# Stores of y issued by ScalarE, and raw rows of the operand preparation queued behind the latest weights

## The chip, the core and the metric

The kernel runs on one core of one Trainium2 chip. The time is device microseconds of one execution of the whole program. Five engines work side by side, each from its own queue in order: TensorE (PE; PEld is its loading of weights), VectorE (DVE), ScalarE (ACT), GpSimd (POOL) and SyncE (SP), which in this kernel issues every transfer.

## What is computed

One layer of a hybrid decoder block over 2048 tokens of width 1024, in float32, followed by a gated projection of a second input p and a final norm. Cut to what matters:

```
z = rmsnorm(h, norm_mix) @ w_in                     # 1024 -> 5392 columns
aq, ak, av, gq, gk, gv, g_low, za, zg = split(z)
y_att = swa_sink_attention(rope(aq), rope(ak), av, sinks)   # 16 heads of 64, window 128
o     = gla_chunked(gq, gk, gv, logsigmoid(g_low @ w_gate_up + b_gate) / 16)  # 4 heads
y     = concat(y_att * silu(za), rmsnorm(o, gla_norm) * silu(zg))   # 2048 wide
h     = h + y @ w_out
gate  = sigmoid(rmsnorm(h, ple_norm) @ w_ple_gate)
out   = rmsnorm(h + gate * (p @ w_ple_proj), final_norm)
```

## The kernel before

Every product is split into a high and a low part of float32r, three matmuls for one (`gemm`, line 83: high by high, high by low, low by high). Hence each weight tile has two buffers, `wh` and `wl`.

The tokens are worked in two halves of eight tiles of 128. In each half the normalised input stays on the chip (`uth`, `utl`), and column groups of w_in pass by one after the other. Section A makes keys, values and the low-rank gate input of each tile. Then, for each of four GLA heads i, come `v_block`, `qk_block` and eight GLA tiles (`gla_tile`, line 549), and behind heads 0, 1 and 2 come the attention groups 0 and 1, 2, and 3, eight attention tiles each (`att_tile`, line 409). An attention tile goes from projection and rotary through scores (`s`), exponentials, transposes (`pq`) and the product with values to `oy` on VectorE (line 479), which is stored to the DRAM scratch `yts[t]` (line 480). A GLA tile ends in a transpose and ScalarE's copy to `oyg` (line 586), stored by line 587. These are 64 stores each of 128 KB.

`load_w` (line 265) brings one column group into one of two buffer slots (`wps`). In the first half raw columns come from w_in, and ScalarE and GpSimd split them into `wh` and `wl`, which are also saved to DRAM (`wd`, line 292). In the second half the saved parts come back with eight transfers, `wh` and `wl` in turn (lines 278 and 279).

Only in the second half there runs, between the tiles, the generator `right_operands` (line 597). It prepares the operands of the output products, which use a seven-product scheme for 2x2 blocks: 48 units, each with four raw rows loaded into `rb` (line 609), four differences on VectorE (`tm`), splits on ScalarE (`th`, line 625) and GpSimd (line 626), and four stores to `td` (line 628). Its tiles come from the pool `rawp` (nine buffers).

The program text gives only the order in which work is traced. The tile framework simulates the engines when the program is built and lays out each engine's queue by when it takes each instruction to be ready. `tc.issue_after(ins)` (line 607) adds a rule to that: what is traced in its block on the engine of `ins` stands behind `ins` in that engine's queue, without waiting for it to finish. `pace[0]` holds that instruction; before the change it is the store of y that was traced last (lines 480 and 587). `tick` (line 308) advances all open generators by one step between blocks of projection.

Behind the second half follow the output products (`products`, line 780) with operands `T` loaded from `td` (line 122) and y read back from `yts` (line 805).

Of the kernel before, what the change touches and what calls it, by code (L numbers as in the profile page):

```python
# [10 lines left out]
F32 = mybir.dt.float32  # L11
# [27 lines left out]
def hybrid_block_kernel(  # L39
# [5 lines left out]
    nc = tc.nc  # L45
# [4 lines left out]
    yts = [dram.tile([P, 16, P], F32, name=f"yts{t}") for t in range(NT)]  # L50
# [5 lines left out]
    def pt(tag, shape=(P, 512), dtype=F32, bufs=2):  # L56
        return psum.tile(list(shape), dtype, name=tag, tag=tag, bufs=bufs)
# [68 lines left out]
    with ExitStack() as p1:  # L126
# [27 lines left out]
        def w1(name, dtype=F32, shape=(P, 256)):  # L154
            return wk.tile(list(shape), dtype, name=name, tag="w1", bufs=8)
# [91 lines left out]
        def rope(q, nh, t):  # L247
            cb = csC[:, t, :].unsqueeze(1).broadcast_to([P, nh, 16])
            s0 = csS[:, t, 0:8].unsqueeze(1).broadcast_to([P, nh, 8])
            s1 = csS[:, t, 8:16].unsqueeze(1).broadcast_to([P, nh, 8])  # L250
            a = wk.tile([P, 4, 16], F32, name="ra", tag="ra", bufs=1)[:, 0:nh, :]
            b = wk.tile([P, 4, 16], F32, name="rb", tag="rb", bufs=1)[:, 0:nh, :]
            dve.tensor_tensor(a, q[:, :, 0:16], cb, op=ALU.mult)
            dve.tensor_tensor(b[:, :, 0:8], q[:, :, 8:16], s0, op=ALU.mult)
            dve.tensor_tensor(b[:, :, 8:16], q[:, :, 0:8], s1, op=ALU.mult)
            dve.tensor_tensor(q[:, :, 0:16], a, b, op=ALU.add)
# [4 lines left out]
        slot = [0]  # L261

        wds = {}

        def load_w(cols, fast=False):
            n = sum(c[1] for c in cols)
            wp = wps[slot[0] % 2]
            slot[0] += 1
            wh = wp.tile([P, KD, SW], F32R, name="wh", tag="wh")
            wl = wp.tile([P, KD, SW], F32R, name="wl", tag="wl")  # L270
            key = tuple(cols)
            saved = wds.get(key)
            if saved is None:
                wds[key] = dram.tile([P, 2, KD, n], F32, name=f"wd{len(wds)}")
            for k0 in range(0, KD, 2):
                ks_ = slice(k0, k0 + 2)
                if saved is not None:
                    nc.sync.dma_start(wh[:, ks_, 0:n].bitcast(F32), saved[:, 0, ks_, :])
                    nc.sync.dma_start(wl[:, ks_, 0:n].bitcast(F32), saved[:, 1, ks_, :])
                    continue  # L280
                raw = rawp.tile([P, 2, SW], F32, name="raw", tag="raw")
                o = 0
                for c0, m in cols:
                    nc.sync.dma_start(raw[:, :, o:o + m], w_v[:, ks_, c0:c0 + m])
                    o += m
                act.activation(wh[:, ks_, 0:n], raw[:, :, 0:n], AF.Copy)  # L286
                eng = dve if fast and k0 % 4 == 0 else pool
                eng.tensor_tensor(wl[:, ks_, 0:n], raw[:, :, 0:n], wh[:, ks_, 0:n], op=ALU.subtract)  # L288
            if saved is None:

                for i, part in enumerate((wh, wl)):
                    nc.sync.dma_start(wds[key][:, i], part[:, :, 0:n].bitcast(F32))
            return wh, wl

        def tok_gemm(ps, w, lt, c0, n):
            ts_ = slice(lt * P, lt * P + P)
            gemm(ps[:, 0:n], lambda k: uth[:, k, ts_], lambda k: utl[:, k, ts_],
                 lambda k: w[0][:, k, c0:c0 + n], lambda k: w[1][:, k, c0:c0 + n], KD)
# [110 lines left out]
        def att_tile(half, g, wq, lt, szas):  # L409
            kv = g // 2  # L410
            t = half * HT + lt
            ps = pt("acc")
            tok_gemm(ps, wq, lt, 0, 256)
            q = w1("q", shape=(P, 4, 64))
            act.activation(q, ps[:, 0:256].rearrange("p (h d) -> p h d", h=4), AF.Copy)
            rope(q, 4, t)
            stk = w2("stk", F32R, (P, 4, 2, 64))
            split(stk[:, :, 0, :], stk[:, :, 1, :], q)
            yield
            tp = pt("t", dtype=F32R)  # L420
            for j in range(4):
                pe.transpose(tp[:, j * P:(j + 1) * P], stk[:, j].rearrange("p a d -> p (a d)"), identr)
            qT = w2("qT", F32R, (P, 4, P))
            act.activation(qT, tp.rearrange("p (h n) -> p h n", h=4), AF.Copy)
            yield
            sp = pt("s", (P, 4, 256), bufs=1)
            win = slice(lt * P, lt * P + 256)
            for j in range(4):
                pe.matmul(sp[:, j, :], qT[:, j, :], kT[:, kv, 0, win], start=True, stop=False)
                pe.matmul(sp[:, j, :], qT[:, j, :], kT[:, kv, 1, win], start=False, stop=True)  # L430
            s = w2("s", F32, (P, 4, P))
            act.activation(s, sp[:, :, P:256], AF.Copy)
            um = umask.unsqueeze(1).broadcast_to([P, 4, P])
            if t == 0:
                dve.copy_predicated(s, um, negc.unsqueeze(2).broadcast_to([P, 4, P]))
            else:
                dve.copy_predicated(s, um, sp[:, :, 0:P])
            hsl = slice(4 * g, 4 * g + 4)
            sm = wk.tile([P, 6, 4], F32, name="sm", tag="sm", bufs=3)
            mx, ng, es, su, dn = (sm[:, i, :] for i in range(5))  # L440
            dve.tensor_reduce(out=mx, in_=s, op=ALU.max, axis=AX.X)
            dve.scalar_tensor_tensor(ng, mx, -1.0, nsk[:, hsl], op0=ALU.mult, op1=ALU.min)  # L442
            dve.tensor_tensor(es, ng, nsk[:, hsl], op=ALU.subtract)
            act.activation(es, es, AF.Exp)
            for j in range(4):
                act.activation(s[:, j, :], s[:, j, :], AF.Exp, bias=ng[:, j:j + 1], accum_out=su[:, j:j + 1])  # L446
            dve.tensor_tensor(dn, su, es, op=ALU.add)
            dve.reciprocal(dn, dn)
            dve.scalar_tensor_tensor(s, s, 0.5, dn.unsqueeze(2).broadcast_to([P, 4, P]),
                                     op0=ALU.mult, op1=ALU.mult)  # L450
            yield
            yield
            tp = pt("t")
            for j in range(4):
                pe.transpose(tp[:, j * P:(j + 1) * P], s[:, j, :], ident)
            pq = kvp.tile([P, 4, 512], F32R, name="pq", tag="pq", bufs=1)
            split(pq[:, 0, :], pq[:, 1, :], tp)
            pmb = pmask.unsqueeze(1).broadcast_to([P, 4, P])
            for i in range(2):
                pool.tensor_tensor(pq[:, 2 + i, :].rearrange("p (h n) -> p h n", h=4),  # L460
                                   pq[:, i, :].rearrange("p (h n) -> p h n", h=4), pmb, op=ALU.mult)
            yield
            yield
            po = pt("o")
            vp = vs[:, lt, kv].rearrange("p a d -> p (a d)")
            vq = vd[:, lt, kv].rearrange("p a d -> p (a d)")
            pe.matmul(po, vp, pq[:, 0, :], start=True, stop=False)
            pe.matmul(po, vp, pq[:, 1, :], start=False, stop=False)
            pe.matmul(po, vq, pq[:, 2, :], start=False, stop=False)
            pe.matmul(po, vq, pq[:, 3, :], start=False, stop=True)  # L470
            pv = po.rearrange("p (a b n) -> p a b n", a=2, b=2)
            ot = w1("ot", shape=(P, 2, P))
            act.activation(ot[0:64], pv[64:128, :, 0, :], AF.Copy)
            act.activation(ot[64:128], pv[0:64, :, 1, :], AF.Copy)
            dve.tensor_tensor(ot[0:64], ot[0:64], pv[0:64, :, 0, :], op=ALU.add)
            dve.tensor_tensor(ot[64:128], ot[64:128], pv[64:128, :, 1, :], op=ALU.add)
            oy = w1("oy", shape=(P, 2, P))
            l2 = lt % 4
            dve.tensor_tensor(oy, ot, szas[lt // 4][:, :, l2 * P:(l2 + 1) * P], op=ALU.mult)
            pace[0] = nc.sync.dma_start(yts[t][:, 2 * g:2 * g + 2, :], oy).ins  # L480


        def gla_gates(half, h, sub, res):
# [65 lines left out]
        def gla_tile(half, h, wz, lt, ops):  # L549
            t = half * HT + lt  # L550
# [33 lines left out]
                pe.transpose(tq[:, j * P:(j + 1) * P], y[:, j * P:(j + 1) * P], ident)  # L584
            oy = w1("oyg", shape=(P, 2, P))
            act.activation(oy, tq[:, 0:256].rearrange("p (a n) -> p a n", a=2), AF.Copy)
            pace[0] = nc.sync.dma_start(yts[t][:, 8 + 2 * h:10 + 2 * h, :], oy).ins

        pace = [None]

        def run_chain(c):
            next(c)
# [497 lines left out]
```

## Time and profile before

| what | value |
|---|---|
| median of 3 runs | 1906.24 us (1900.41 to 1909.64) |
| profiled execution | 1904.04 us, its span 1902.3 us |
| mean granted TensorE clock | 0.990 |
| TensorE, VectorE, ScalarE, GpSimd busy | 95%, 63%, 51%, 37% |
| transfers | 326.78 MB, mean 172 GB/s |

How to read it: busy shares are over the whole span, which has parts of different kinds; a wait is the time in which an engine stood idle, put down to what released it last. An engine that isn't the bound may stand idle at no cost. SyncE's rows are issues: the time is that of the issuing instruction, and the data lands some us later.

### The profile page before, as it was taken

Reading aid. Unit: us, or ns where it says so; the run is one execution under the profiler, and the core shown is the slowest. Engines: PE = TensorE matmul, PEld = TensorE weight load, DVE = VectorE, ACT = ScalarE, POOL = GpSimd, SP = SyncE. Lnnn points to the kernel's source line nnn. Section 1 sums busy time; section 2 is a strip of 40 time slices with the busy share of each in tenths; the row PEclk is TensorE's granted clock in tenths of the full one; section 3 lists DMA queues with packets and bytes.
Section 4 is the critical chain, followed back from the end, with each engine's and each line's share of the span. In section 5 each row is a group of like instructions: output and inputs, shape, how many; then the busy total and the mean of one; then the engine's idle time right before and its main releaser. Section 6 shows DMA issues by size and latency. Waiting matters only on the chain. (4 is left out here: it accounts for less than half of the span.)

```text
span 1902.3 us, 32715 instructions
## 1 busy us (share of the span) xinstructions
PE 1814.7 (95%) x11297; PEld 1612.9 (85%) x11297; DVE 1203.3 (63%) x2663; ACT 961.1 (51%) x2598; POOL 699.3 (37%) x916
## 2 busy tenths in 40 slices
PE   6999999999999999999999999999899999998997
PEld 6989898998898889898888988988788888787886
DVE  6454785466556474578766756574667667665864
ACT  5544666465557464456654655563422244453543
POOL 5442554534526362544455445352200010102432
PEclk9999999999999999999999999999999999999998
DMA  8332442415324352655576566565685966884542
GB/s 281 122 101 81 147 136 92 155 53 170 97 66 143 102 180 90 199 146 174 178 205 206 163 195 182 160 195 192 230 281 194 324 237 219 313 309 151 179 139 83
DMA packets 326741, 326.78 MB, mean 172 GB/s; under 512 B 23137, under 2 KB 259825, under 8 KB 326321
## 3 DMA queue, kind: packets, MB, share of 16 engines
q1 hardware_dynamic: 326576, 324.70, 52.5%
q8 instruction: 89, 1.46, 0.3%
q14 instruction: 76, 0.61, 0.1%
HBM read 186.08 MB, written 138.54 MB: 171 GB/s over the span
## 5 line engine op out<-in xcount | busy, mean ns | idle before, releaser
L85 PE MATMUL acc<-wh,uth 128*128 128x256 f32 (+1 forms) x1664 | 476.8, 287 | 14.5 <-DVE m L563 4.5
L86 PE MATMUL acc<-wl,uth 128*128 128x256 f32 (+1 forms) x1664 | 472.6, 284 | 6.2 <-DMA wl<-wd 6.0
L87 PE MATMUL acc<-wh,utl 128*128 128x256 f32 (+1 forms) x1664 | 471.1, 283 | 0.0
L85 PEld LDWEIGHTS acc<-wh,uth 128*128 128x128 f32 x1664 | 316.0, 190 | 25.6 <-ACT v L522 5.9
L86 PEld LDWEIGHTS acc<-wl,uth 128*128 128x128 f32 x1664 | 315.7, 190 | 12.9 <-DMA wl<-wd 8.6
L87 PEld LDWEIGHTS acc<-wh,utl 128*128 128x128 f32 x1664 | 315.7, 190 | 2.0
L460 POOL TENSOR_TENSOR pq<-pq,pmask 128x512 fp32r<-128x512 f32 x128 | 178.2, 1408 | 292.9 <-ACT pq L67 285.8
L85 PE MATMUL acc<-uth,wh 128*128 128x512 f32 x512 | 204.3, 399 | 4.8 <-DVE m L563 3.8
L87 PE MATMUL acc<-uth,wl 128*128 128x512 f32 x512 | 201.7, 394 | 0.3 <-DMA wl<-wd 0.3
L86 PE MATMUL acc<-utl,wh 128*128 128x512 f32 x512 | 201.9, 394 | 0.0
L774 PE MATMUL acc<-T,c 128*128 128x512 f32 (+1 forms) x344 | 135.5, 395 | 6.7 <-ACT u L829 6.3
L775 PE MATMUL acc<-T,c 128*128 128x512 f32 (+1 forms) x344 | 135.1, 393 | 0.0
L776 PE MATMUL acc<-T,c 128*128 128x512 f32 (+1 forms) x344 | 135.0, 393 | 0.0
L446 ACT ACTIVATE s<-s,sm 128x128 f32<-128x128 f32 x256 | 99.7, 391 | 51.1 <-DVE sm L442 51.1
L85 PEld LDWEIGHTS acc<-uth,wh 128*128 128x128 f32 x512 | 96.4, 188 | 26.8 <-DVE m L563 5.2
L859 POOL TENSOR_TENSOR ssh<-ssh 128x1 f32<-128x1 f32 x16 | 3.3, 205 | 313.8 <-ACT junk L858 313.8
L288 POOL TENSOR_TENSOR wl<-raw,wh 128x512 fp32r<-128x512 f32 (+1 forms) x82 | 109.6, 1367 | 20.0 <-ACT wh L286 10.2
L87 PEld LDWEIGHTS acc<-uth,wl 128*128 128x128 f32 x512 | 96.1, 188 | 22.5 <-DMA wl<-wd 0.7
L86 PEld LDWEIGHTS acc<-utl,wh 128*128 128x128 f32 x512 | 96.2, 188 | 18.7
L67 ACT ACTIVATE c<-s 128x512 fp32r<-128x512 f32 x72 | 45.1, 629 | 111.1 <-DVE s L104 32.4
L774 PE MATMUL o<-T,c 128*128 128x512 f32 (+1 forms) x252 | 99.3, 394 | 0.0
L775 PE MATMUL o<-T,c 128*128 128x512 f32 (+1 forms) x252 | 98.6, 391 | 0.0
(289 smaller groups left out, 4409.7 us busy)
## 6 DMA issues: line engine op xcount, KB each, us to landing
T<-td SPq DMA_DIRECT2D x84, 512.0 KB, 9.4
wd<-wh SPq DMA_DIRECT2D x20, 1024.0 KB, 5.6
wd<-wl SPq DMA_DIRECT2D x20, 1024.0 KB, 6.3
wh<-wd SPq DMA_DIRECT2D x80, 256.0 KB, 5.4
wl<-wd SPq DMA_DIRECT2D x80, 256.0 KB, 5.5
raw<-in_w_in SPq DMA_DIRECT2D x68, 256.0 KB, 5.6
y<-yts SPq DMA_DIRECT2D x64, 256.0 KB, 5.6
td<-th SPq DMA_DIRECT2D x48, 256.0 KB, 2.8
```

What stands on the lines that cost most here:

```text
L67: act.activation(h, src, AF.Copy)
L85: pe.matmul(ps, lhs_h(k), rhs_h(k), start=(k == 0), stop=False)
L86: pe.matmul(ps, lhs_h(k), rhs_l(k), start=False, stop=False)
L87: pe.matmul(ps, lhs_l(k), rhs_h(k), start=False, stop=(k == nk - 1))
L288: eng.tensor_tensor(wl[:, ks_, 0:n], raw[:, :, 0:n], wh[:, ks_, 0:n], op=ALU.subtract)
L446: act.activation(s[:, j, :], s[:, j, :], AF.Exp, bias=ng[:, j:j + 1], accum_out=su[:, j:j + 1])
L460: pool.tensor_tensor(pq[:, 2 + i, :].rearrange("p (h n) -> p h n", h=4), pq[:, i, :].rearrange("p (h n) -> p h n", h=4), pmb, op=ALU.mult)
L774: pe.matmul(ps, c[:, 0, k, :], t[:, 0, k, sl], start=(first and k == 0), stop=False, skip_group_check=more)
L775: pe.matmul(ps, c[:, 0, k, :], t[:, 1, k, sl], start=False, stop=False, skip_group_check=more)
L776: pe.matmul(ps, c[:, 1, k, :], t[:, 0, k, sl], start=False, stop=(k == 3), skip_group_check=more)
L859: pool.tensor_tensor(ss[:, 0:1], ss[:, 0:1], ss[:, 1:2], op=ALU.add)
```

## The change

The stores of `oy` and `oyg` are issued from ScalarE's queue instead of SyncE's. `pace[0]` is now the last transfer of `wl` from saved weights that was traced, so a unit's raw rows stand in SyncE's queue behind that one instead of behind the last store of y.

```diff
         wds = {}
+        pace = [None]
 
         def load_w(cols, fast=False):
...
                 if saved is not None:
                     nc.sync.dma_start(wh[:, ks_, 0:n].bitcast(F32), saved[:, 0, ks_, :])
-                    nc.sync.dma_start(wl[:, ks_, 0:n].bitcast(F32), saved[:, 1, ks_, :])
+                    pace[0] = nc.sync.dma_start(wl[:, ks_, 0:n].bitcast(F32), saved[:, 1, ks_, :]).ins
                     continue
...
             dve.tensor_tensor(oy, ot, szas[lt // 4][:, :, l2 * P:(l2 + 1) * P], op=ALU.mult)
-            pace[0] = nc.sync.dma_start(yts[t][:, 2 * g:2 * g + 2, :], oy).ins
+            nc.scalar.dma_start(yts[t][:, 2 * g:2 * g + 2, :], oy)
...
             act.activation(oy, tq[:, 0:256].rearrange("p (a n) -> p a n", a=2), AF.Copy)
-            pace[0] = nc.sync.dma_start(yts[t][:, 8 + 2 * h:10 + 2 * h, :], oy).ins
-
-        pace = [None]
+            nc.scalar.dma_start(yts[t][:, 8 + 2 * h:10 + 2 * h, :], oy)
```

## Rows read from the trace of the kernel before

**Rows 1.** The page: busy us, share of the span and instructions of each engine.

```profile
span 1902.3 us, 32715 instructions
PE 1814.7 (95%) x11297; PEld 1612.9 (85%) x11297; DVE 1203.3 (63%) x2663; ACT 961.1 (51%) x2598; POOL 699.3 (37%) x916
```

**Rows 2.** Table by stretch: length, busy PE, PEld, DVE, ACT, POOL; clock; DMA share; GB/s.

```profile
100.00:650.00 550.00, 535.27 (x3686) 489.75 (x3687) 332.65 (x782) 306.60 (x915) 250.45 (x269) 1.00 0.34 110
800.00:1345.00 545.00, 519.34 (x3534) 471.12 (x3533) 356.97 (x924) 299.93 (x892) 249.81 (x263) 0.99 0.60 179
```

**Rows 3.** TensorE's waits, whole span: us in total, times, longest us.

```profile
PE o L525 <- ACT sh L67: 8.6, 10, 2.5
PE acc L85 <- DVE m L563: 8.3, 9, 1.8
...
PE acc L86 <- DMA wl<-wd: 6.0, 7, 2.5
...
PE o L467 <- ACT pq L67: 3.2, 5, 1.5
PE acc L85 <- DMA wh<-wd: 2.8, 5, 0.9
...
PE o L525 <- ACT kt L67: 2.3, 3, 1.8
```

**Rows 4.** SyncE in order of time, near 925 us: start us, us, issues.

```profile
922.75 0.36 SPq L278 DMA_DIRECT2D wh<-wd  x1
923.53 0.33 SPq L480 DMA_DIRECT2D yts<-oy  x1
923.92 2.97 SPq L609 DMA_DIRECT2D rb<-in_w_out  x4
...
927.46 0.43 SPq L279 DMA_DIRECT2D wl<-wd  x1
```

**Rows 5.** TensorE in order of time, near 931 us; in brackets idle time before, releaser.

```profile
931.47 0.38 PE L86 MATMUL acc<-wl,uth 128*128 128x256 f32 x1 [2.53 <-DMA wl<-wd]
```

**Rows 6.** SyncE in order of time, near 1125 us.

```profile
1121.37 0.36 SPq L279 DMA_DIRECT2D wl<-wd  x1
1124.02 0.33 SPq L480 DMA_DIRECT2D yts<-oy  x1
1124.40 1.88 SPq L609 DMA_DIRECT2D rb<-in_w_ple_gate  x4
...
1128.25 0.50 SPq L278 DMA_DIRECT2D wh<-wd  x1
```

**Rows 7.** Table by stretch again, behind the two gaps; the clock is third from last.

```profile
932.00:940.00 8.00, 7.56 (x47) 6.90 (x46) 5.39 (x17) 3.47 (x13) 3.53 (x4) 0.79 1.06 347
1142.00:1150.00 8.00, 6.89 (x38) 6.13 (x39) 8.00 (x18) 7.02 (x18) 6.60 (x10) 0.79 0.87 245
```

**Rows 8.** SyncE's waits, 800 to 1345 us.

```profile
SPq L278 <- PE acc L87: 24.4, 4, 13.5
```

**Rows 9.** TensorE in order of time, 1141 to 1145 us.

```profile
1141.95 0.38 PE L525 MATMUL o<-vv,kt 128*128 128x256 f32 x1 [1.78 <-ACT kt L67]
...
1144.09 0.39 PE L525 MATMUL o<-sh,qq 128*128 128x256 f32 x1 [1.06 <-ACT sh L67]
```

**Rows 10.** Issues of y stores by line: ns min/median/max, first and last start.

```profile
L587 SPq DMA_DIRECT2D yts<-oyg x64: 319/349/1230, 118.0 to 1357.9; - x64
L480 SPq DMA_DIRECT2D yts<-oy x64: 319/332/1453, 186.5 to 1297.5; - x64
```

**Rows 11.** ScalarE and SyncE in order of time, pieces of two tiles.

```profile
463.79 0.38 ACT L474 ACTIVATE ot<-o 64x256 f32<-64x256 f32 x1
...
466.14 0.38 SPq L480 DMA_DIRECT2D yts<-oy  x1
...
1344.54 0.38 ACT L586 ACTIVATE oyg<-t 128x256 f32<-128x256 f32 x1
1344.81 0.28 ACT L67 ACTIVATE kt<-t 128x128 fp32r<-128x128 f32 x1
```

## What I expect of the change, and how it is worked out

> **What bounds the kernel now.** I read the page's busy line first [rows 1]: TensorE has work for 1814.7 of 1902.3 us, ScalarE for 961.1, so only what leaves TensorE idle, or lowers its clock, sets the end. Then a table by stage [rows 2]. In the stretch of the first half that holds only projection, attention and GLA (100 to 650 us) TensorE idles 550 - 535.27 = 14.7 us. In the same work of the second half (800 to 1345 us) it idles 545 - 519.34 = 25.7 us, and the mean granted clock is 0.99 there instead of 1.00. What follows is the output products, which the change doesn't edit. So the second half pays some 11 us and a little clock more, and the question is what is in it and not in the first: saved weights that come back from DRAM, and the operand preparation.
>
> The list of TensorE's waits names it [rows 3]: 6.0 us in 7 places for wl and 2.8 us in 5 for wh, 8.8 us in sum. The other four rows there are waits for ScalarE, or for VectorE work that follows ScalarE: sh, m and kt in GLA tiles (10 + 9 + 3 = 22 places), pq in attention tiles (5 places). Those are where a slower ScalarE queue would show.
>
> Why are weights late? SyncE's queue in order of time tells it. At 922.75 us it issues the first wh piece; then come a store of y and four raw rows (2.97 us), and the first wl piece leaves at 927.46 [rows 4]. TensorE stands 2.53 us for that piece, until 931.47 [rows 5]. At 1121.37 a wl piece leaves, then SyncE stands until a store of y can go at 1124.02, gives four raw rows the next 1.88 us, and the wh pieces begin at 1128.25 [rows 6]. So both things that the change moves stood in front of weights. The granted clock falls behind each of the two gaps in TensorE's work: its mean is 0.79 in the 8 us that follow, a mixture of the 1.2 and the 2.4 GHz level [rows 7].
>
> **The change, part by part.** *Gain in the second half.* The wl waits, 6.0 us, I count as gone: with stores off the queue, and raw rows traced later put behind the weights, nothing but the stores of the preparation is left to stand between a wh piece and its wl. Of the wh waits, 2.8 us, I count half, 1.4 us, since a weight buffer must first be released by TensorE; SyncE waited 24.4 us in four places for exactly that [rows 8]. The clock behind the two gaps: 2 x (1 - 0.79) x 8 us = 3.4 us. Sum 6.0 + 1.4 + 3.4 = 10.8 us. Bounds: 0, if other work of SyncE stands before the weights instead; at the top 8.8 + 3.4 + 1.8 + 1.1 = 15.1 us, with the two waits for kt and sh that TensorE has within 10 us of the second gap [rows 9]. Next to be late after the weights are those ScalarE chains in any case.
>
> *Cost of 128 stores on ScalarE's queue.* ScalarE issues no transfer in this trace, so I price one by SyncE's: 64 stores of attention tiles at 0.332 us and 64 of GLA tiles at 0.349 us in the median, up to 1.45 [rows 10]. That is 21.2 + 22.3 = 43.6 us for a queue whose engine is busy 306.60 + 299.93 = 606.5 of 1095 us in the two stretches, 55% [rows 2]. A GLA store waits for ScalarE's own copy to oyg. In one tile the copy takes 0.38 us and the next activation starts 0.27 us after it [rows 11]; a store right behind it makes ScalarE drain, 0.11 us, and costs 0.35 + 0.11 = 0.46 us. Behind it stand the kt, sh, at and qq pieces and the gate m of the neighbouring tiles. If each of the 22 places were hit in full: 22 x 0.46 = 10.1 us. In 45% of the time ScalarE has nothing to do and a store fills idle time: 10.1 x 0.55 = 5.6 us. An attention store is written by VectorE, so nothing drains, and 0.33 us of issue is shorter than a copy already under way (0.38 us, [rows 11]). I take 0 for it; its bound is that attention tiles become as close as GLA tiles, 22 x 0.33 = 7.3 us. Cost 5.6 us, bounds 0 and 10.1 + 7.3 = 17.4 us. The first half pays its share of this and gains nothing, since its weights are made on the chip and TensorE has no weight wait there.
>
> *SyncE and buffers.* SyncE loses 43.6 us of issues and its waits for finished tiles. It isn't the bound, so this alone is worth nothing beyond the weights. Buffers of y come free sooner when stores leave at once; no wait of TensorE in [rows 3] is for one, so 0.
>
> *Raw rows.* All 48 x 4 = 192 stay on SyncE, 1.88 / 4 = 0.47 us each in [rows 6]. Now a group of four leaves right behind a store of y [rows 4, 6], so the preparation keeps step with the tiles. After the change rows need only weights before them and a free buffer, and the preparation can run in bursts behind each set of weights. A burst costs VectorE, ScalarE and GpSimd work beside attention, whose most exposed piece is pq, 3.2 us in 5 places [rows 3]. Bounds: 0, and as much again, 3.2 us; I take 0, as pieces come at any time already now and these waits are few.
>
> *Transition to the output products.* The last eight stores move to ScalarE with the rest, among the first splits of that stage, 8 x 0.35 = 2.8 us beside transfers of operands that TensorE awaits there: 0.
>
> **Sum.** -10.8 + 5.6 = -5.2 us. The profiled execution took 1904.04 us (span 1902.3, [rows 1]), 2.2 under the median of the runs, 1906.24; from 1904.04 the sum gives 1898.8, and with those 2.2 us 1901.0 us.
>
> A rule of the Trainium skill speaks against the change, in sentences of their own. "Perfetto Trace Analysis", section "DMA Instruction — HWDGE (DVE, Sync)", says that a sequencer locks the descriptor generator for its exclusive use, so an issue of ScalarE would stand while SyncE issues. No run here shows it yet, since only SyncE issues; rival 4 is the same mechanism priced from rows.
>
> **The rivals.** (1) *ScalarE hides the stores, and the weights come fully on time.* For it: 45% idle on ScalarE, and the two gaps have visible causes. Against: 22 places where TensorE follows ScalarE without slack. 1906.2 - 15.1 = 1891.1 us.
>
> (2) *ScalarE is held by the attention store (slower).* The store needs oy, which VectorE finishes after two additions and whatever stands between. In one tile the second copy to ot starts on ScalarE at 463.79 us, ends 0.38 later, and SyncE issues the store at 466.14 [rows 11], 2.0 us after the end. If the store stands right behind that copy, ScalarE stands 2.0 us with the next tile's copies, exponentials and pq behind it, and TensorE behind those. TensorE is close behind ScalarE in 5 of 64 attention tiles and 22 of 64 GLA tiles, 0.08 and 0.34; I take the middle, 0.2, so a held tile costs 0.4 us. Slower than before from 5.2 / 0.4 = 13 held tiles on, by over 0.5% from (5.2 + 9.5) / 0.4 = 37 of the 64; two thirds of them give 1901.0 + 17 = 1918 us. Against it: between copy and store there is room for other pieces of ScalarE's queue.
>
> (3) *It doesn't do what it says.* Weights stay late, because their buffers come free late [rows 8] or because stores of the preparation, which nothing in the change holds back, stand before them. Half the wl waits gained, 3.0 us, 5.6 paid: 1908.8 us.
>
> (4) *Two issuing queues take turns.* If a store on ScalarE stood for one issue of SyncE, 0.47 us as a raw row takes, the GLA places would cost 22 x (0.46 + 0.47) x 0.55 = 11.3 us and eat the gain: 1906.7 us.
>
> **How the numbers follow.** Forecast 0.40, rival 1 0.28, rival 2 0.15, rival 3 0.10, rival 4 0.07. A change of 0.5% (9.5 us: outside 1896.7 to 1915.8) is about what a measurement of this kernel can tell from none; the three runs of before lie between 1900.41 and 1909.64. Faster: rival 1 and 0.05 of the forecast's lower edge, 0.33. Slower: rival 2 and 0.04 of the forecast's upper edge, 0.19. Same: the rest, 0.48. The range takes in the forecast with its bounds (1906.2 - 15.1 = 1891.1 to 1906.2 + 17.4 = 1923.6, of which the last 4 us need every bound at once), rival 1 with 4 us of scatter, and the lower part of rival 2: 1887 to 1920 us.
>
> **What would show it.** Right: TensorE's waits for wl and wh fall to under 3 us and the two dips of the clock are gone; in SyncE's order a wl piece follows its wh without raw rows between; TensorE's idle time of the second half nears the first's. The step on ScalarE: waits for sh, m and kt grow by some 6 us in sum, over both halves. Wrong: a large row of ScalarE waiting for oy (rival 2); the weights' row stays (rival 3); an issue on ScalarE lasts 0.8 us or more in the median (rival 4); TensorE's waits for pq grow (bursts).

## The result, and the profile after

The changed kernel takes 1927.2 us in the median against 1907.7 for the kernel before, beside it on the same chip: a ratio of 1.0107, 95% interval 1.0080 to 1.0134. It is slower, and above the range of the forecast. The profiled execution took 1927.23 us, its span is 1925.5 us, 23.2 us longer than in [rows 1].

The page's busy line and the table by stretch, with the columns of [rows 2]:

```profile
PE 1824.5 (95%) x11297; PEld 1622.5 (84%) x11297; DVE 1230.1 (64%) x2663; ACT 962.1 (50%) x2598; POOL 691.4 (36%) x916
```

```profile
100.00:650.00 550.00, 531.41 (x3662) 486.72 (x3662) 336.44 (x781) 305.37 (x909) 247.00 (x267) 1.00 0.33 109
650.00:800.00 150.00, 138.28 (x984) 128.93 (x983) 80.13 (x201) 73.18 (x202) 62.71 (x136) 0.95 0.48 150
800.00:1345.00 545.00, 516.30 (x3487) 468.73 (x3486) 377.40 (x920) 299.84 (x886) 243.16 (x263) 0.98 0.59 178
```

The same 11297 matmuls keep TensorE busy 9.8 us longer than in [rows 1], so of the 23.2 us some 13.4 are idle time and 9.8 are work that takes longer; the granted clock is lower where that happens.

TensorE's idle time in the first half grew from 14.7 to 18.6 us, in the late stretch of the second half from 25.7 to 28.7, with the clock at 0.98 instead of 0.99. The stretch between, 650 to 800 us, which the prediction hadn't looked at, now idles 11.7 us at a mean clock of 0.95.

TensorE's waits (us in total, times, longest us), the rows that answer to [rows 3] and the one for VectorE's part of pq:

```profile
PE o L526 <- ACT sh L67: 11.6, 10, 3.4
...
PE o L469 <- DVE pq L68: 7.2, 8, 1.7
PE o L468 <- ACT pq L67: 6.4, 7, 1.7
...
PE acc L85 <- DVE m L564: 4.5, 4, 1.1
...
PE o L526 <- ACT kt L67: 2.0, 3, 1.2
...
PE acc L86 <- DMA wl<-wd: 1.0, 3, 0.4
...
PE acc L85 <- DMA wh<-wd: 0.5, 1, 0.5
```

The waits for weights fell from 8.8 to 1.5 us, as the forecast had it. The waits for pq grew most: by ScalarE from 3.2 to 6.4 us, and for VectorE's part of it to 7.2 us. In the kernel before, that row is:

```profile
PE o L468 <- DVE pq L68: 1.2, 3, 0.5
```

The waits for sh grew from 8.6 to 11.6 us; those for m fell. SyncE has time to spare now: between 800 and 1345 us it stands for weight buffers that TensorE hasn't yet released, where [rows 8] had 24.4 us:

```profile
SPq L279 <- PE acc L87: 123.1, 6, 29.9
```

To see where the 23 us arise, I read from the order in time of VectorE and ScalarE when four pieces end that every version has: the 32nd oy (the end of the first half's attention), the 16th kst (the end of section A in the second half), the 33rd oyg (the first GLA tile of the second half) and the 64th oy. The table gives the us between them; each value is a difference of two ends, and each row is one execution: that of before lies some 4 us under the median of its runs, that of the pace only 5.7 us over its own. Runs named here are told of below.

| run | to 32nd oy | to 16th kst | to 33rd oyg | to 64th oy | to the end |
|---|---|---|---|---|---|
| before | 619.3 | 113.7 | 37.6 | 524.4 | 607.3 |
| changed | 624.4 | 113.6 | 49.7 | 532.6 | 605.2 |
| control | 621.7 | 114.6 | 37.6 | 523.2 | 605.0 |
| pace only | 621.1 | 113.7 | 48.4 | 542.6 | 607.0 |
| first rows early | 626.2 | 117.2 | 46.6 | 529.6 | 606.6 |
| both paces | 620.6 | 113.8 | 39.3 | 527.4 | 604.9 |
| changed, pieces in order | 625.7 | 112.9 | 38.6 | 517.5 | 606.3 |
| pace only, pieces in order | 620.6 | 113.9 | 38.3 | 522.3 | 608.8 |
| before, pieces in order | 621.2 | 113.1 | 38.2 | 520.8 | 608.0 |
| first half's stores on ScalarE | 624.2 | 118.1 | 37.6 | 526.5 | 609.6 |
| the same, GLA stores only | 620.4 | 119.5 | 37.6 | 526.9 | 608.6 |

The changed kernel loses 5.1 us in the first half, 12.1 us within the first GLA head of the second half, 8.2 us up to the last attention tile, and gets 2.1 us back. The first column scatters by 2.4 us (619.3 to 621.7) among the runs that don't have attention stores on ScalarE.

**The 12 us.** Order of time in the changed kernel (SyncE, VectorE, ScalarE, TensorE; in brackets the idle time before, and what ended it):

```profile
735.74 0.38 SPq L280 DMA_DIRECT2D wl<-wd  x1
...
746.61 6.49 SPq L608 DMA_DIRECT2D rb<-in_w_out  x8
...
761.95 2.60 SPq L608 DMA_DIRECT2D rb<-in_w_out  x4
...
753.36 0.29 DVE L104 TENSOR_TENSOR tm<-rb 128x128 f32<-128x128 f32 x1 [4.02 <-DMA rb<-in_w_out]
...
757.27 0.68 DVE L516 TENSOR_TENSOR qk<-acc,em 128x512 f32<-128x512 f32 x1
...
753.93 0.53 ACT L624 ACTIVATE th<-rb 128x384 fp32r<-128x384 f32 x1 [6.57 <-DMA rb<-in_w_out]
...
761.93 0.52 ACT L624 ACTIVATE th<-rb 128x384 fp32r<-128x384 f32 x1 [3.06 <-DMA td<-th]
...
762.92 0.40 ACT L67 ACTIVATE sh<-sd 128x256 fp32r<-128x256 f32 x1
...
758.01 0.33 PE L536 MATMUL t<-identr,qk 128*128 128x128 f32 x1 [1.24 <-DVE qk L516]
...
763.37 0.58 PE L526 MATMUL o<-sh,qq 128*128 128x256 f32 x1 [3.37 <-ACT sh L67]
```

SyncE begins 16 weight transfers of 256 KB at 735.74 us and only then, at 746.61, the first raw rows of the preparation. The preparation's pieces then stand at the heads of two queues: VectorE 4.0 us and ScalarE 6.6 us for rows in flight. Behind VectorE's stands qk, and TensorE waits 1.24 us for it. The rows of further units follow without a pause, the fourth unit's at 761.95. ScalarE stands another 3.1 us, for a store of the preparation that still holds the buffer of the third unit's piece; behind that piece stand kt and sh of the GLA tiles, and TensorE waits 3.37 us.

The first units alone aren't the price. In the run with both paces, told of below, their rows also leave right behind these weights and ScalarE stands for them as long, but the fourth unit's rows wait for the store of the first GLA tile:

```profile
742.71 7.01 SPq L610 DMA_DIRECT2D rb<-in_w_out  x8
...
750.38 0.53 ACT L626 ACTIVATE th<-rb 128x384 fp32r<-128x384 f32 x1 [6.96 <-DMA rb<-in_w_out]
...
774.09 2.77 SPq L610 DMA_DIRECT2D rb<-in_w_out  x4
```

There the stretch takes 39.3 us, 1.7 more than before. The rest of the 12 us comes with the units that follow at once. In the kernel before there is no unit's work in this stretch: the first three units' rows leave in section A, from 695.49 us on, and the fourth's wait for the store of y that comes at the end of the stretch, until 771.03.

The clock then makes it dearer (table by stretch; the clock is third from last):

```profile
762.00:766.00 4.00, 2.63 (x12) 2.61 (x12) 3.32 (x10) 3.91 (x12) 3.04 (x5) 0.50 0.86 242
...
778.00:782.00 4.00, 4.00 (x13) 3.32 (x13) 3.89 (x11) 2.55 (x9) 3.47 (x5) 0.50 0.71 202
...
738.00:787.70 49.70, 42.33 (x230) 37.08 (x229) 29.07 (x65) 25.81 (x61) 23.93 (x33) 0.86 0.78 227
```

0.50 is the level of 1.2 GHz throughout a slice. The last line is the whole stretch from the 16th kst to the 33rd oyg. In the kernel before it is:

```profile
733.00:770.60 37.60, 36.98 (x232) 32.47 (x231) 17.62 (x41) 19.65 (x51) 8.44 (x20) 1.00 0.32 105
```

TensorE idles 7.4 us instead of 0.6 and is busy 42.3 instead of 37.0 us with the same work, at a mean clock of 0.86: 6.7 + 5.4 = 12.1 us.

Over the whole span, the waits of ScalarE (th) and VectorE (tm) for raw rows. The kernel before has 12.1 + 11.3 and 9.9 + 9.0 us there, the run with both paces 30.9 and 23.4 without being slower; the changed kernel has 47.5 and 29.9 us:

```profile
ACT th L624 <- DMA rb<-in_w_out: 31.0, 13, 6.6
...
DVE tm L104 <- DMA rb<-in_w_out: 21.1, 20, 4.0
...
ACT th L624 <- DMA rb<-in_w_ple_gate: 16.5, 9, 3.8
...
DVE tm L104 <- DMA rb<-in_w_ple_gate: 8.8, 7, 2.5
```

Where the 8.2 us up to the last attention tile arise, piece by piece, wasn't followed; the runs below show what they depend on.

**The 5 us of the first half.** ScalarE and TensorE near the end of an attention group:

```profile
444.67 0.33 ACTq L481 DMA_DIRECT2D yts<-oy  x1
445.05 0.60 ACT L433 ACTIVATE s<-s 128x512 f32<-128x512 f32 x1 [1.76 <-DVE oy L480]
...
452.56 0.50 PE L469 MATMUL o<-pq,vs 128*128 128x512 f32 x1 [1.69 <-DVE pq L68]
```

ScalarE stands 1.76 us until VectorE has made oy, and the next tile's copy of the scores is behind the store. What follows from it, exponentials and pq, is late, and TensorE stands 1.69 us; before, its longest stand in that part was 0.30 us. It stands as long again at 607.17 us, and the mean clock from 608 to 616 us is 0.79, where before had 1.00. ScalarE's waits for oy over the whole span, the two largest rows:

```profile
ACT v L523 <- DVE oy L480: 6.5, 4, 2.1
...
ACT s L433 <- DVE oy L480: 3.5, 2, 1.8
```

With two smaller rows they are 12.8 us in 8 places, 4 of these in the first half. The store itself takes (ns min/median/max, first and last start):

```profile
L588 ACTq DMA_DIRECT2D yts<-oyg x64: 326/327/1056, 117.7 to 1381.0; - x64
L481 ACTq DMA_DIRECT2D yts<-oy x64: 325/326/384, 186.2 to 1322.3; - x64
```

### The profile page after: what moved, and what is told of

The parts are those of the page before. It is cut to its first block, busy times and chain, and to the rows that moved or that the text cites. A ratio compares the mean times of both kernels' runs of the same rounds, so it can differ in the third digit from the quotient of the medians.

```text
span 1925.5 us, 32675 instructions
## 1 busy us (share of the span) xinstructions
PE 1824.5 (95%) x11297; PEld 1622.5 (84%) x11297; DVE 1230.1 (64%) x2663; ACT 962.1 (50%) x2598; POOL 691.4 (36%) x916
## 5 line engine op out<-in xcount | busy, mean ns | idle before, releaser
L85 PE MATMUL acc<-wh,uth 128*128 128x256 f32 (+1 forms) x1664 | 478.5, 288 | 11.3 <-DVE m L564 4.5
```

Of the source, the lines that this page charges most:

```text
L85: pe.matmul(ps, lhs_h(k), rhs_h(k), start=(k == 0), stop=False)
```

## The experiments

Three theories stood at the start: H, ScalarE is held by stores of oy; P, the looser pace lets the preparation run where it stood still, with its pieces in front of tile work; S, the framework plans all queues anew after any edit, and the time scatters by that.

**One part alone, and a control.** First half only on ScalarE:

```diff
-            pace[0] = nc.sync.dma_start(yts[t][:, 2 * g:2 * g + 2, :], oy).ins
+            if half == 0:
+                nc.scalar.dma_start(yts[t][:, 2 * g:2 * g + 2, :], oy)
+            else:
+                pace[0] = nc.sync.dma_start(yts[t][:, 2 * g:2 * g + 2, :], oy).ins
...
+                    pace[0] = lastw[0]
```

The store of a GLA tile is edited alike; `lastw[0]` is the last transfer of wl that was traced.

> Only the 64 stores of the first half go to ScalarE; the second half keeps its stores on SyncE and its pace behind stores of y (the first two units behind the weights of the first value projection, since no store of y stands on SyncE yet). Theory H (held ScalarE: a store of oy in ScalarE's queue stands until VectorE has made oy): the loss of the changed kernel by the end of the first half's attention, 5 us against before at the 32nd oy, is here in full and nothing beyond it: 1907.7 + 5 = 1912 to 1914 us. Theory P (pace: the time of the raw rows is the main loss): the same 5 us, and the 18 us of the second half are gone. Theory S (scatter of the plan): any time within 10 us of before, and the 32nd oy not 5 us late.

Measured: ratio 1.0052 (1.0031 to 1.0073), 1919.6 us. The 32nd oy is 4.9 us late, as in the changed kernel. But a second loss came with it, 4.4 us in section A of the second half, which the changed kernel doesn't have: with its first units' raw rows freed early, they leave at 685.20 us instead of 695.49, and TensorE idles 8.2 us there against 5.9 at a mean clock of 0.97. It is a small case of P that my edit made itself: the run with the first rows early, below, differs from the changed kernel by nothing else and loses 3.6 us there. After it the times run within some 2 us of before's, so the second half's 18 us are gone.

Pace alone, all stores on SyncE:

```diff
-                    nc.sync.dma_start(wl[:, ks_, 0:n].bitcast(F32), saved[:, 1, ks_, :])
+                    pace[0] = nc.sync.dma_start(wl[:, ks_, 0:n].bitcast(F32), saved[:, 1, ks_, :]).ins
...
-            pace[0] = nc.sync.dma_start(yts[t][:, 2 * g:2 * g + 2, :], oy).ins
+            nc.sync.dma_start(yts[t][:, 2 * g:2 * g + 2, :], oy)
```

> Only the pace is changed: raw rows behind the latest weights; all stores of y stay on SyncE. Theory P: the second half loses what it lost in the changed kernel, 12 us in the first GLA head of the second half and some 6 more in attention: 1907.7 + 18 = 1922 to 1927 us. Theory H: the loss needs stores on ScalarE, so at most a few us remain: 1900 to 1912 us. Where raw rows follow weights, waits for wl and wh fall to about 1.5 us by both.

Measured: 1.0109 (1.0077 to 1.0141), 1928.9 us. The pace alone makes a loss as large as the whole change, 20.0 us by the medians. In the profiled execution, 5.7 us over the median, 10.8 us lie between the 16th kst and the 33rd oyg and 18.2 us between that and the 64th oy. ScalarE's waits for raw rows:

```profile
ACT th L624 <- DMA rb<-in_w_out: 28.0, 14, 6.1
...
ACT th L624 <- DMA rb<-in_w_ple_gate: 24.0, 7, 9.9
```

TensorE's waits for wl and wh fell to 2.0 us here too, although the stores of y still stand on SyncE: that row follows the pace and not the stores.

The changed kernel with the first two units' raw rows let go earlier:

```diff
-                with tc.issue_after(pace[0]):
+                with tc.issue_after(pace0 if first else pace[0]):
...
+                    pace0 = pace[0]
```

`pace0` is the last transfer of the value projection's weights.

> The changed kernel, but the raw rows of the first two units stand behind the weights of the value projection instead of behind the 16 transfers of the qk and z weights. Theory P in its narrow form (the 12 us between 735 and 770 us come from the first raw rows, which land late behind those 4 MB while ScalarE and VectorE stand at the pieces that need them): 10 to 12 us come back, 1927 - 11 = 1914 to 1918 us. Theory H: unchanged, 1925 to 1929 us, since the stores on ScalarE are the same. If the second units only burst later, 5 us come back.

Measured: 1.0100 (1.0067 to 1.0132), 1929.1 us. The narrow form of P falls. The first rows came in time, and the stretch to the 33rd oyg still took 46.6 us: the rows of five more units leave between 752 and 775 us, as in the changed kernel. Section A took 3.6 us more instead.

The control:

```diff
     act.activation(warm, mhalf, AF.Square)
+    act.activation(warm, mhalf, AF.Square)
```

> Control: the kernel before with one more activation of one column on ScalarE at the very start (0.2 us of work), so that the queues are planned anew with no cause in the second half. Theories H and P: within 3 us of before, 1905 to 1911 us. Theory S (the plan scatters by as much as the change moved): 10 us or more off in either direction.

Measured: 1.0004 (0.9983 to 1.0026). But the framework didn't plan anew: in the trace every engine has before's instructions in before's order, with the one added in front. So the control shows how far executions of the same queues scatter, 2.4 us in the table's columns, and doesn't test S. What speaks against S is the other runs: the kernel before with pieces in order, below, has widely reordered queues and moves by 0.2%, and the three runs with the loose pace and no tie, the changed kernel among them, lie 1.0 to 1.1% above before, the nine others between 0.5% below and 0.7% above.

**Two ways to take the preparation out of the way.** Raw rows behind both the latest store of y and the latest weights:

```diff
+                    wpace[0] = nc.sync.dma_start(wl[:, ks_, 0:n].bitcast(F32), saved[:, 1, ks_, :]).ins
...
-                with tc.issue_after(pace[0]):
+                with tc.issue_after(pace[0]), tc.issue_after(wpace[0]):
```

> All stores of y on SyncE as before; raw rows behind the latest store of y and behind the latest weights as well. Theory P (loosening the pace lets the preparation run where before it stood still, and its pieces stand in front of tile work while their raw rows are still on the way): the old rule still holds, so none of the 12 us in the first GLA head nor the loss after it: 1900 to 1910 us, with the waits for wl and wh under 3 us. If being behind the weights is itself the harm (rows that land late behind 4 MB), the loss stays: over 1920 us.

Measured: 0.9996 (0.9982 to 1.0010), 1908.7 us. The loss is gone. In the trace SyncE's order differs from before's in one thing only: the rows of the first three units, with the first two units' stores, leave behind the 16 weight transfers instead of in section A. So for these units being behind the weights is no harm, and what the changed kernel lost comes of units that no longer wait for stores of y. The second half of the expectation failed: the waits for wl and wh stayed at 7.8 + 0.9 = 8.7 us, as the rest of SyncE's order stayed.

The changed kernel with the preparation's pieces tied to the place where they are traced:

```diff
-                diff(dve, tm[:, 1], r[:, 0], r[:, 1])
+                tc.keep_in_program_order(dve.tensor_tensor(tm[:, 1], r[:, 0], r[:, 1], op=ALU.subtract))
...
-                    act.activation(h, src, AF.Copy)
+                    tc.keep_in_program_order(act.activation(h, src, AF.Copy))
```

The tie is to one piece, the one traced last before it on that engine, not to all before it, as my expectations put it.

> The changed kernel, but each unit's first and last difference on VectorE and its two copies on ScalarE are pinned behind everything traced before them on their engine, so they can't be planned ahead of earlier tile work; raw rows are paced as in the changed kernel and stores stay on ScalarE. Theory P: the 12 us between 735 and 770 us and most of the later loss come back, 1927 - 15 = 1909 to 1915 us, with the 5 us of the first half left. If rows in flight hurt by their transfers alone (weights late, engines of the DMA full): no gain, 1922 us or more.

Measured: 0.9971 (0.9954 to 0.9989), 1903.3 us: 24 us faster than the changed kernel, with its pace and its stores on ScalarE unchanged, and with the 5 us of the first half still in it. The tie also spreads the raw rows: the fourth unit's begin at 778.66 us instead of 761.95. So this run doesn't part the stand at the heads of the queues from the transfers and the work of the burst. The table by stretch, and ScalarE's wait for raw rows:

```profile
650.00:800.00 150.00, 145.13 (x1080) 136.08 (x1079) 82.46 (x210) 75.86 (x216) 62.65 (x144) 1.00 0.43 137
800.00:1345.00 545.00, 525.55 (x3592) 477.15 (x3590) 369.51 (x945) 304.35 (x909) 257.98 (x276) 1.00 0.62 184
```

```profile
ACT th L624 <- DMA rb<-in_w_out: 8.5, 2, 6.0
```

The clock is at 1.00 in both stretches of [rows 7], and TensorE idles 19.5 us from 800 to 1345 us against 25.7 before the change. But the waits for weights are back, 6.1 + 1.4 + 0.6 us in 12 places, with no store of y on SyncE:

```profile
PE acc L86 <- DMA wl<-wd: 6.1, 9, 1.8
...
PE acc L85 <- DMA wh<-wd: 1.4, 2, 1.1
```

SyncE's order ahead of the longest of them, TensorE's wait itself, and the stretch behind it:

```profile
1084.18 0.36 SPq L627 DMA_DIRECT2D td<-rb  x1
1084.63 1.40 SPq L608 DMA_DIRECT2D rb<-in_w_out  x3
...
1087.50 0.40 SPq L279 DMA_DIRECT2D wh<-wd  x1
1087.99 0.41 SPq L627 DMA_DIRECT2D td<-th  x1
1088.50 0.44 SPq L280 DMA_DIRECT2D wl<-wd  x1
...
1093.23 0.52 PE L86 MATMUL acc<-wl,uth 128*128 128x256 f32 x1 [1.84 <-DMA wl<-wd]
...
1092.00:1100.00 8.00, 6.77 (x42) 6.51 (x43) 4.32 (x14) 3.04 (x8) 2.50 (x2) 0.79 1.05 330
```

Raw rows and the preparation's own stores stand there. The rule puts rows behind the weights traced before them, and nothing keeps them from standing in front of the next weights. Behind this wait the clock dips as it did in [rows 7].

The same tie with the stores on SyncE:

> Stores of y on SyncE, raw rows behind the latest weights, and the preparation's differences and copies pinned in traced order. Theory P: against the run with the pace alone (1928.9 us) 18 us or more come back, and with weights on time it may beat before: 1898 to 1910 us. Rival: stores of y on SyncE stand before weights still, so waits for wl and wh stay at some 5 us and the time at 1908 to 1915 us.

Measured: 0.9953 (0.9935 to 0.9971), 1901.9 us, the lowest median of all, though its interval overlaps those of the other two runs with the tie. The waits for weights, 6.8 + 6.6 us, didn't fall either.

And the same tie in the kernel before:

> The kernel before (stores on SyncE, raw rows behind the latest store of y) with the preparation's differences and copies pinned in traced order. Theory P: before has little of this harm (its raw rows wait behind stores of y, and the preparation stands still in the first GLA head), so pinning brings it only the few us that it brings the two others beyond their loss: 1898 to 1908 us, against 24 us that the changed kernel got back. If pinning were a gain of its own that has nothing to do with the pace, it would bring some 24 us here too: 1885 us.

Measured: 0.9979 (0.9965 to 0.9993), 1903.7 us. The tie brings 4 us where the pace was tight and 24 to 27 us where it was loose. With the tie, three versions with either pace and either issuer lie within 1901.9 to 1903.7 us. So the issuer by itself makes no difference that can be told over the whole kernel: with the loose pace, ScalarE and SyncE give 1.0107 and 1.0109, with the tie besides 0.9971 and 0.9953. What stores on ScalarE cost in the first half they seem to give back in the second (with the tie 517.5 against 522.3 us to the 64th oy); that is read from one execution of each.

**Where ScalarE's 5 us lie.** Only the 32 GLA stores of the first half on ScalarE (of the edit above, the attention store goes back to SyncE):

> As the run with the first half's stores on ScalarE, but of these only the 32 stores of GLA tiles; the attention stores of the first half stay on SyncE. Theory H (attention stores hold ScalarE in front of the copy of the scores): the 5 us by the 32nd oy are gone (621 us or less). The forecast's own step said the opposite, that the cost sits at GLA stores: then some 2 to 3 us stay. Beyond the first half nothing else than in that run: 1912 to 1916 us in all.

Measured: 1.0020 (1.0006 to 1.0034), 1912.2 us; the 32nd oy ends at 620.4 us, within the scatter of the runs without stores on ScalarE. So the attention stores cost some 4 us by then, and the 32 GLA stores nothing that can be seen. The loss that is left has its largest part, 5.8 us in the profiled execution, in section A, where my edit makes it.

Then three attempts to keep the attention store on ScalarE and move it. One step later:

```diff
-                nc.scalar.dma_start(yts[t][:, 2 * g:2 * g + 2, :], oy)
+                yield
+                tc.keep_in_program_order(nc.scalar.dma_start(yts[t][:, 2 * g:2 * g + 2, :], oy))
```

> As the run with the first half's stores on ScalarE, but the store of an attention tile is traced one step later and pinned behind all that is traced on ScalarE before it, so that ScalarE doesn't reach it before VectorE has made oy. Theory H: the 5 us that the first half lost by its 32nd oy are gone, 1919.6 - 5 = 1913 to 1916 us, and the 32nd oy within 1.5 us of the control's. If the 0.33 us issue itself is the cost, 5 us stay.

Measured: 1.0043 (1.0028 to 1.0059), the 32nd oy at 624.8 us. The edit hardly moved the store:

```profile
445.08 0.33 ACTq L485 DMA_DIRECT2D yts<-oy  x1
445.45 0.60 ACT L435 ACTIVATE s<-s 128x512 f32<-128x512 f32 x1 [1.77 <-DVE oy L482]
```

Three steps later, the same way:

> As the run with the first half's stores on ScalarE, but an attention store is traced three steps later and pinned behind all that is traced on ScalarE before it (one step later hadn't moved it: ScalarE still stood 1.77 us for oy in front of the next tile's copy of the scores). Theory H: ScalarE's waits for oy in the first half, 6.2 us in 4 places, vanish, and with them the 5 us by the 32nd oy: that falls within 2.5 us of before's 619.3, and the time is 1912 to 1916 us. If the issue itself costs them, the 32nd oy stays at 624.

Measured: 1.0071 (1.0045 to 1.0097), the 32nd oy at 624.5 us, with the same stand of 1.77 us. Neither run moved the store, so neither tells anything about H. At last behind the copy of the scores:

```diff
-            act.activation(s, sp[:, :, P:256], AF.Copy)
+            copied[0] = act.activation(s, sp[:, :, P:256], AF.Copy).ins
...
+                with tc.issue_after(copied[0]):
+                    nc.scalar.dma_start(yts[t][:, 2 * g:2 * g + 2, :], oy)
```

> As the run with the first half's stores on ScalarE, but each attention store is traced three steps later and queued behind the latest copy of the scores on ScalarE. (A pin behind the piece traced last before it had not moved the store: ScalarE still stood 1.77 us for oy in front of that copy.) Theory H: the wait of 1.77 us in front of the copy vanishes, TensorE's 1.65 us for pq near 452 and 607 us with it, and the 32nd oy is within 2 us of before's 619.3. If the issues themselves cost the time, it stays at 624.

Measured: 1.0063 (1.0036 to 1.0091), the 32nd oy at 625.9 us. The stand in front of the copy is gone, and TensorE's waits for VectorE's part of pq there fell from 4.1 us to 1.4 us in four places. Yet the time didn't come back. Two stores now stand together behind the copy, in front of the next GLA head's gate pieces:

```profile
445.96 0.60 ACT L436 ACTIVATE s<-s 128x512 f32<-128x512 f32 x1
445.97 1.62 ACTq L488 DMA_DIRECT2D yts<-oy  x2
447.63 0.69 ACT L497 ACTIVATE e<-acc,bg 128x512 f32<-128x512 f32 x1 [1.07 <-DMA yts<-oy]
```

So it is shown that the attention stores on ScalarE's queue cost some 4 us of the first half. That the stand for oy in front of the scores is the price is what the trace says of the changed kernel; moving it only made another. How it divides between the stand and the issue stays open.

## Why the prediction was wrong

- *The bound*: right. TensorE's idle time and clock set the time, and the 23.2 us are found there, 13.4 us idle and 9.8 us of slower work.
- *Gain at the weights, 10.8 us*: the rows fell as forecast, from 8.8 to 1.5 us, but not for the reason given and without a gain in time. With the pace alone they fell too, to 2.0 us, though the stores of y stayed where they were; with the stores moved and the preparation spread out they are back at 8.1 us. They are small in the three runs with the loose pace and no tie, and 7.7 us or more in every other. The trace of the changed kernel says why: the preparation runs in bursts and leaves SyncE free in between (123.1 us of waits for buffers), and the bursts are what costs the time. The three fastest runs have late weights, 8.1 to 13.4 us. The step took the two visible neighbours for the cause; rival 3 had the preparation's own stores in it, which do stand there, with raw rows beside them. The clock's 3.4 us went from the two places named and came back elsewhere: in the changed kernel behind the bursts, in the run with pieces in order at 1092 us.
- *GLA stores on ScalarE, 5.6 us*: mis-sized. 32 of them in the first half cost nothing that can be seen, and the waits for sh, m and kt, which were to grow by some 6 us, went from 19.2 to 18.1 us.
- *Attention stores, taken as 0*: wrong; some 4 us in the first half. The bound of 7.3 us held it. The reason for 0, that an issue is shorter than an activation under way, left out that ScalarE stands until oy is there. Rival 2 had the mechanism: a stand of 1.76 us against its 2.0. It had the wrong weights, though: ScalarE stood in 8 of 64 tiles, where the rival needed 13 to be slower at all, and the four stands of the first half go with some 4 us, about 1 us each and not 0.4. Not this made the kernel slower.
- *Raw rows, 0 with a bound of 3.2 us*: this is the step that failed. It costs some 20 us (20.0 by the medians with the pace alone; 12.1 + 8.2 in the table). The sentence "pieces come at any time already now" was not looked up: before, raw rows leave right behind a store of y, so the preparation stood still from 703 to 771 us, up to the end of the first GLA tile. The bound was taken from ScalarE's part of pq alone, and not from what a burst does: unit behind unit at the heads of ScalarE's and VectorE's queues, in front of kt, sh and qk, and TensorE at the lower clock behind the gaps. How the price divides between the stands for data, the pieces' own work and the transfers stays open. And of the pace I had asked what it puts in front of the weights, and not what it had held back.
- *Rival 4, two issuers in turn*: out. "Perfetto Trace Analysis" of the Trainium skill, section "DMA Instruction — HWDGE (DVE, Sync)", has a sequencer lock the descriptor generator for itself. Here the issue on ScalarE took 0.327 and 0.326 us in the median, no longer than SyncE's 0.349 and 0.332 in [rows 10]; one GLA store took 1.06 us. The measurement decides: no price of that size is to be seen.
- *The signs named in advance*: the weights' rows and the growing waits for pq were read rightly beforehand as "right" and as "bursts". They came together, which the cases, each by itself, hadn't allowed for.

## What to carry to other kernels

A rule of order that looks like a brake on one queue may be what keeps later work off the heads of the others. Before loosening it, look in the trace for the stretches where the braked work stands still now, and ask what stands behind its pieces in each queue while its data is in flight. And see whether a row that falls does so for the reason you had: here the weights came on time because of the bursts that cost more. If a transfer is to be let go earlier, tie the pieces that consume it to their place: that was worth 24 us here, against 4 us where the brake was still on.

## What the runs showed of the hardware that I had not expected

Units of the preparation, run one behind the other after 16 weight transfers, left TensorE idle for 7.4 of 49.7 us, but the granted clock fell to 0.50 in two slices of 4 us and its mean over the stretch to 0.86, and the same work took 5.4 us longer. Over the whole span the slower work is 9.8 us beside 13.4 us of added idle time, so waits added up from a trace show little more than half of the loss. A mean over a long stretch hides such places: in the run with the pieces in order the table shows 1.00 from 800 to 1345 us, and 0.79 from 1092 to 1100.
